# Projection products that read the two token tiles in turn

## The chip, the cores and the metric

The kernel runs on one core of one Trainium2 chip. The time is device microseconds of one execution, given as the median of several runs. Lower is better. A core has TensorE (matrix products, PE in the profile, with its weight loads as PEld), VectorE (DVE), ScalarE (ACT), GpSimd (POOL) and SyncE (SP, which issues most transfers here). Products are written to PSUM, and VectorE and ScalarE read them there.

## The reference

Two decoder layers over 256 tokens of width 1024, and a final RMSNorm. The whole is float32.

```python
h = rms_norm(x, gain)
proj = h @ w_in                       # 1024 x 9808: q, k, v, gate of three mixers, index, merge gates
# three causal mixers, 8 heads of 64 each: a block attention (one block here), an indexer that picks
# the top 64 keys of each query, and forgetting attention; a and b rotate 16 of 64 dims by position
oa, ob, oc = attention_n(q, k, v) * silu(gate)
y = stack([oa, ob, oc]) @ w_branch    # 512 x 1024 each
merged = sum(sigmoid(merge_logit) * y)
x = x + merged @ w_out                # 1024 x 1024
```

## The kernel before

**Numbers in two parts.** Every operand of a product is split into a high part of type fp32r and a rest (`wh`, `wl` for weights; `hTh`, `hTl` for the normalised input; `q`, `bd`, `og` and so on likewise), and a product of two such operands is three products on TensorE: high by high, high by low, low by high. ScalarE makes the high part with a copy, VectorE the rest with a subtraction.

**Two kinds of projection.** For v and the output, `unit_a` has the tokens as the stationary side and 512 weight columns as the moving side. For everything else (q, k, gates, index, merge gates), `unit_b` has 128 weight columns stationary and all 256 tokens moving, so that the result is transposed: features in partitions, tokens in columns. Such a unit is 24 products of 128 x 128 by 256 (8 chunks of the width, three products each) into one PSUM buffer `proj`, of which there are three. `unit_y`, the branch output, is the same with 12 products over `og`. Over both layers there are 130 units of 24 products (two of them with 80 weight columns, `kwf`) and 48 units of 12. All are issued by `mm_ops` (L403); its operands are `hTh[:, k]` or `og[..][:, k]`, 256 consecutive fp32r columns, of which 0 to 127 are the first tile of tokens and 128 to 255 the second.

**Readers of `proj`.** Merge gates: a tanh on ScalarE (L817, L820). Mixer gates: tanh, then a product with `proj` on VectorE (`ev_g`). q and k of mixers a and b and the index: `rope` with two tables from `cst` (`rope_t`), a shuffle and a product on VectorE and two steps on POOL, result in `rr`; then a split, by `split_to` into `q` or by `write_bd` into `bd`, a block-diagonal pair of heads. q and k of mixer c: the split reads PSUM directly. The branch outputs are multiplied with the merge gates into `acc`, which is split into `merged` after the third (`mg`). `kwf` holds the index key and 16 columns that go to `wf`.

**Attention of a pair of heads** (`attend`): the scores `s` (L569 to L571) read `q` by tiles of 128 tokens as stationary side and `bd` as moving side; softmax on VectorE and ScalarE; transposes (L659); products with v into `o` (L674 to L677); then `gated` multiplies `ot` with the gate `g` on POOL or VectorE (L694, L695) and splits into `og`. Scores, masks and transposes are done tile by tile and need tokens in plain order.

**Order.** Nothing is scheduled by the compiler. `Plan.run` replays a list of operations with costs and fixes each engine's order when the program is built; at run time each engine executes its list in that order with semaphores. Weights arrive by DMA into `raw` (three buffers) and are split at L358 (ScalarE) and L362 (VectorE) into rings `wh` and `wl`. At the end stands a block `forms()` whose products go to unused PSUM buffers and reach no output: several ways to read or write a product, after all others on TensorE (L1054 to L1066), beside the final norm's last steps.

The access of the test at L1064, `a` being 128 and `b` two, visits columns 0, 128, 1, 129, ...:

```python
for i in range(4):
    PE.matmul(b2[:, :256].rearrange("p (a b) -> p a b", a=128), w(i), c(i).rearrange("p (b a) -> p a b", a=128), start=True, stop=True)
```

L1054 is the plain read, L1056 a plain read of bf16, L1058 and L1060 read every second column, L1062 every sixteenth, L1066 a plain read from column 8 on.

Of the kernel before, what the change touches and what calls it, by code (L numbers as in the profile page):

```python
# [11 lines left out]
AF = mybir.ActivationFunctionType  # L12
ALU = mybir.AluOpType

L = 2
S = 256
# [3 lines left out]
KC = D // 128  # L20
# [31 lines left out]
def shape_constants():  # L52
    c = np.zeros((128, C_END), np.float32)
    i = np.arange(128)
    c[:, C_ID:C_ID + 128] = np.eye(128)
    c[:, C_UT:C_UT + 128] = i[:, None] <= i[None, :]
    diag = np.where(i[None, :] <= i[:, None], 0.0, MASKED)
    c[:, C_MASK:C_MASK + 128] = diag
    c[:, C_MASK + 256:C_MASK + 384] = diag
    inv = np.power(np.float32(500000.0), -np.arange(0, 16, 2, dtype=np.float32) / np.float32(16))  # L60
    ang = np.arange(S, dtype=np.float32)[None, :] * inv.astype(np.float32)[:, None]
    cos, sin = np.cos(ang).astype(np.float32), np.sin(ang).astype(np.float32)
    ct = np.ones((128, S), np.float32)
    st = np.zeros((128, S), np.float32)
    for b in (0, 64):
        ct[b:b + 8] = cos
        ct[b + 8:b + 16] = cos
        st[b:b + 8] = -sin
        st[b + 8:b + 16] = sin
    c[:, C_ROPE:C_ROPE + 256] = ct  # L70
    c[:, C_ROPE + 256:C_ROPE + 512] = st
    c[:, C_ROPE + 512:C_ROPE + 768] = ct * np.float32(-0.125)
    c[:, C_ROPE + 768:C_ROPE + 1024] = st * np.float32(-0.125)
    return c
# [142 lines left out]
def t_dve(n):  # L217
    return 68.0 + n / 0.96
# [6 lines left out]
def t_pool(n):  # L225
    return 250.0 + 2.2 * n
# [7 lines left out]
def hybrid_trunk(ctx, tc, x, norm_gain, w_in, forget_bias, w_branch, w_out, final_gain, consts, out):  # L234
# [7 lines left out]
    plan = Plan()  # L242
# [7 lines left out]
    def T(b):  # L250
        return b.slot[1]
# [30 lines left out]
    gT = pool.tile([128, L, KC], F32, name="gT")  # L282
    hTh = pool.tile([128, KC, S], F32R, name="hTh")
    hTl = pool.tile([128, KC, S], F32R, name="hTl")
    og = [[pool.tile([128, 4, S], F32R, name=f"og{i}{p}") for p in "hl"] for i in range(2)]
    NBD = 3
    bd = [[pool.tile([128, 2, S], F32R, name=f"bd{i}{p}") for p in "hl"] for i in range(NBD)]
# [127 lines left out]
    def unit_b(name, get, half=0, npart=128):  # L415

        u = unit(name)
        ps = Buf("proj")
        o = lambda: T(ps)[:npart, :S]
        pp = get(u)  # L420
        n = KC // len(pp)
        w = lambda k, i: pp[k // n][i].v[:, k % n, half * 128:half * 128 + npart]
        his = [(lambda k=k: w(k, 0), lambda k=k, h=h: h[:, k], [pp[k // n][0]] + hT_all[i])
               for k in range(KC) for i, h in enumerate((hTh, hTl))]
        los = [(lambda k=k: w(k, 1), lambda k=k: hTh[:, k], [pp[k // n][1]] + hT_all[0]) for k in range(KC)]
        g = his[:8] + los[:4] + his[8:] + los[4:]
        for a, b in ((0, 8), (8, 12), (12, 20), (20, 24)):
            mm_ops(o, g[a:b], t_mm(256), [ps], u, name, a == 0, b == 24, True)
        return u, ps
# [145 lines left out]
    class Pair:  # L575
# [3 lines left out]
        def ev_q(self, ps, key):  # L579
            q = self.q = (Buf("qh"), Buf("ql"))  # L580
            if self.mixer == "c":
                split_to(lambda: T(q[0]), lambda: T(q[1]), lambda: T(ps)[:, :S], S, True, [ps], q[0], q[1], key,
                         -0.125, "q")
            else:
                r = rope(ps, "q", key)
                split_to(lambda: T(q[0]), lambda: T(q[1]), lambda: T(r), S, False, [r], q[0], q[1], key, name="q")

        def ev_k(self, ps, key):
            self.k, self.kt = new_bd()
# [94 lines left out]
        def gated(self):  # L684
            o, g, key = self.o, self.g, self.o_key
            t = Buf("ot")
            kt = [Tok(), Tok()]
            for h in range(2):
                r = slice(64 * h, 64 * h + 64)
                act(lambda r=r, h=h: ACT.activation(T(t)[r], T(o)[64:, h * S:(h + 1) * S], AF.Copy), S, True,  # L690
                    [o], [kt[h]], key, "og", HALF, touch=[t])
                dve(lambda r=r, h=h: DVE.tensor_tensor(T(t)[r], T(o)[:64, h * S:(h + 1) * S], T(t)[r], op=ALU.add),
                    S, [o], [kt[h]], key, "og", t_dve(S) + HALF, touch=[t])
            plan.op([("POOL", t_pool(S), lambda: POOL.tensor_tensor(T(t), T(t), T(g), op=ALU.mult)),  # L694
                     ("DVE", t_dve(S), lambda: DVE.tensor_tensor(T(t), T(t), T(g), op=ALU.mult))],  # L695
                    [g] + kt, [t], key, 0.0, "og").port = True
            gh, gl = og[self.oi]
            split_to(lambda: gh[:, self.p], lambda: gl[:, self.p], lambda: T(t), S, False, [t],
                     k_og[self.oi][0][self.p], k_og[self.oi][1][self.p], key, 0.5, "og")

    def write_bd(src, b, toks, key, ps, shared=False):
        for h in range(2):
            o = slice(64 * h, 64 * h + 64)
            s = (lambda: T(src)[0:64, :S]) if shared else (lambda o=o: T(src)[o, :S])
            hi = lambda o=o, h=h: T(b)[0][o, h]
            lo = lambda o=o, h=h: T(b)[1][o, h]
            act(lambda hi=hi, s=s: ACT.activation(hi(), s(), AF.Copy), S, ps, [src, k_bdz], [toks[h][0]], key, "bd", HALF, touch=[b])
            dve(lambda hi=hi, lo=lo, s=s: DVE.tensor_tensor(lo(), s(), hi().bitcast(F32), op=ALU.subtract), S,
                [src, toks[h][0]], [toks[h][1]], key, "bd", t_dve(S) + HALF, touch=[b], port=not ps)


    def ev_kwf(l, ps, key):
        act(lambda: ACT.activation(wf[64:80], T(ps)[64:80, :S], AF.Copy), S, True, [ps], [k_wf], key, "wf")
        b, toks = new_bd()
        write_bd(rope(ps, "k", key, 64), b, toks, key, False, shared=True)
        return b, toks
# [48 lines left out]
    def index_scores(p, ps, kb, ktoks, key):  # L765
        q = (Buf("qh"), Buf("ql"))
        r = rope(ps, "k", key)
        split_to(lambda: T(q[0]), lambda: T(q[1]), lambda: T(r), S, False, [r], q[0], q[1], key, name="qi")
        s0, s1 = scores(q, kb, ktoks, key + 1)
        base = (p % 2) * 768  # L770
        rel = [tmp6[:, base:base + 256], tmp6[:, base + 256:base + 768]]
# [57 lines left out]
    def unit_y(l, n, j, oi, gates, rank):  # L829
        u = unit(f"y{n}{j}")  # L830
        p = wbr(l, n, j, u)
        ps = Buf("proj")
        gh, gl = og[oi]
        cs = slice((j % 2) * 128, (j % 2) * 128 + 128)
        o = lambda: T(ps)[:, :S]
        g = []
        for k in range(4):
            wh, wl = lambda k=k: p[0].v[:, k, cs], lambda k=k: p[1].v[:, k, cs]
            g += [(wh, lambda k=k: gh[:, k], [p[0], k_og[oi][0][k]]), (wh, lambda k=k: gl[:, k], [p[0], k_og[oi][1][k]]),
                  (wl, lambda k=k: gh[:, k], [p[1], k_og[oi][0][k]])]  # L840
        g = [g[i] for i in (0, 1, 3, 4, 2, 5, 6, 7, 9, 10, 8, 11)]
        for a in (0, 6):
            mm_ops(o, g[a:a + 6], t_mm(256), [ps], u, f"y{n}{j}", a == 0, a == 6, True)
# [11 lines left out]
        if rank == 2:  # L855
            h, lo = merged(j)
            kh, kl = k_mg[j]
            split_to(lambda: h, lambda: lo, lambda: ac, S, False, [k_acc[j]], kh, kl, u, 0.5, "mg")


    DVE.memset(ones, 1.0)
# [181 lines left out]
    def forms():  # L1043

        b = [Buf(t) for t in "sst"]
        f = hTl.rearrange("p k c -> p (k c)")
        fb, gb = f.bitcast(mybir.dt.bfloat16), hTh.rearrange("p k c -> p (k c)").bitcast(mybir.dt.bfloat16)

        def emit():
            b0, b1, b2 = (T(x) for x in b)  # L1050
            w = lambda i: hTh[:, i, :128]
            c = lambda i: f[:, i * 256:i * 256 + 256]
            for i in range(4):
                PE.matmul(b0[:, :256], w(i), c(i), start=True, stop=True)  # L1054
            for i in range(6):
                PE.matmul(b1[:, :256], gb[:, i * 256:i * 256 + 128], fb[:, i * 512:i * 512 + 256], start=True, stop=True)  # L1056
            for i in range(4):
                PE.matmul(b2[:, :256], w(i), f[:, i * 512:(i + 1) * 512].rearrange("p (c t) -> p t c", t=2)[:, 0], start=True, stop=True)  # L1058
            for i in range(4):
                PE.matmul(b0[:, :256].rearrange("p (a b) -> p a b", a=2), w(i), c(i).rearrange("p (b a) -> p a b", a=2), start=True, stop=True)  # L1060
            for i in range(4):
                PE.matmul(b1[:, :256].rearrange("p (a b) -> p a b", a=16), w(i), c(i).rearrange("p (b a) -> p a b", a=16), start=True, stop=True)  # L1062
            for i in range(4):
                PE.matmul(b2[:, :256].rearrange("p (a b) -> p a b", a=128), w(i), c(i).rearrange("p (b a) -> p a b", a=128), start=True, stop=True)  # L1064
            for i in range(4):
                PE.matmul(b0[:, :256], w(i), f[:, i * 256 + 8:i * 256 + 264], start=True, stop=True)  # L1066
        pe(emit, 3400.0, [k_main] + hT_all[0] + hT_all[1], b, 10 ** 6, "forms")
    forms()
    PLAN_T.append(plan)
    PLAN_T[0] = plan.run({"PE": 0.0, "ACT": 0.0, "DVE": 0.0})  # L1070
# [25 lines left out]
```

## Time and profile before

| | |
|---|---|
| median of 3 runs | 636.49 us (635.48 to 637.81) |
| profiled execution | 635.14 us |
| its span | 633.3 us |
| TensorE busy | 624.4 us, 99% |
| VectorE busy | 543.4 us, 86% |
| ScalarE busy | 395.8 us, 62% |
| GpSimd busy | 86.6 us, 14% |
| TensorE's granted clock | full throughout |
| DMA | 105.56 MB, mean 167 GB/s |

A product's row in the profile is its latency, from its first column to its last result; the next product starts long before that, so busy time hides how closely products follow each other. The chain of work that ended last is followed back from the last instruction, at each step to what released it; its pieces have a start, a length and a count. "x<-y" is written and read tile, without buffer numbers. A row of waits names who waited for whom, the sum in us, how often, and the longest.

### The profile page before, as it was taken

The page shows a single profiled execution, that of the slowest core. Times are in us where ns is not written, and L with a number is a line of the kernel's source. Part 1 is how long each engine was busy: PE and PEld are TensorE (multiplying, and loading weights), DVE is VectorE, ACT ScalarE, POOL GpSimd, SP SyncE. Part 2 cuts the span into 40 slices and gives each one's busy share as a digit, 9 for nine tenths or more (in the row PEclk, how much of TensorE's full clock was granted, in tenths as well). Part 3 has the DMA queues.
Part 4 walks back from the last instruction along what each step waited for, and adds up shares of the span by engine and source line. Part 5 has one row for each costly group of instructions (what it writes and reads, how often), then busy time and mean ns, then how long its engine had stood idle before and what let it go on. Part 6 is the DMA issues. An engine that isn't in the chain of part 4 may idle for free.

```text
span 633.3 us, 12633 instructions
## 1 busy us (share of the span) xinstructions
PE 624.4 (99%) x4866; PEld 595.7 (94%) x4866; DVE 543.4 (86%) x1334; ACT 395.8 (62%) x797; POOL 86.6 (14%) x98
## 2 busy tenths in 40 slices
PE   8999989999999999999999999999999999999999
PEld 7999989899998999999889998998999989999988
DVE  8899998976878989899588999979688798989873
ACT  6775476666756667485486656767566574847641
POOL 1332221100000221200004303020000012221001
PEclk9999999999999999999999999999999999999999
DMA  9844637455472562665555544565736454363701
GB/s 300 278 144 148 200 108 258 135 168 172 148 246 68 170 197 67 200 223 177 154 167 166 181 133 154 176 192 166 232 102 201 128 161 148 117 214 102 265 34 67
DMA packets 93853, 105.56 MB, mean 167 GB/s; under 512 B 4320, under 2 KB 82400, under 8 KB 93792
## 3 DMA queue, kind: packets, MB, share of 16 engines
q1 hardware_dynamic: 93504, 104.36, 51.8%
q8 instruction: 38, 0.62, 0.4%
q10 hardware_dynamic: 288, 0.39, 0.2%
q14 instruction: 23, 0.19, 0.1%
HBM read 103.69 MB, written 1.05 MB: 165 GB/s over the span
## 4 chain that ended last, share of the span: by engine, by line
PE 80%; DVE 16%; ACT 2%; DMA 1%; issue 1%; SPq 0%; ACTq 0%; DVEq 0%
PE proj L403 68%; DVE wl L362 6%; PE t L659 2%; DVE isc L804 2%; PE s L569 1%; PE s L571 1%; PE proj L950 1%; PE s L570 1%; DVE t L803 1%; DMA x<-in_x_dram 1%; DVE isc L783 1%; DVE rsh L451 1%; PE o L677 1%; PE o L674 1%; DVE rr L453 1%
## 5 line engine op out<-in xcount | busy, mean ns | idle before, releaser
L362 DVE TENSOR_TENSOR wl<-raw,wh 128x1024 fp32r<-128x1024 f32 (+1 forms) x190 | 235.5, 1251 | 33.0 <-ACT wh L358 31.1
L403 PE MATMUL proj<-hTh,wh 128*128 128x256 f32 (+1 forms) x1040 | 252.1, 278 | 1.1 <-DVE g L598 1.1
L403 PE MATMUL proj<-hTl,wh 128*128 128x256 f32 (+1 forms) x1040 | 250.9, 277 | 0.0
L358 ACT ACTIVATE wh<-raw 128x1024 fp32r<-128x1024 f32 (+1 forms) x190 | 197.9, 1054 | 79.4 <-PE proj L403 58.5
L403 PEld LDWEIGHTS proj<-hTh,wh 128*128 128x128 f32 (+1 forms) x1040 | 194.7, 187 | 2.5 <-DVE g L598 1.6
L403 PEld LDWEIGHTS proj<-hTl,wh 128*128 128x128 f32 (+1 forms) x1040 | 194.6, 187 | 0.8
L403 PE MATMUL proj<-hTh,wl 128*128 128x256 f32 (+1 forms) x1040 | 163.1, 279 | 0.0
L403 PEld LDWEIGHTS proj<-hTh,wl 128*128 128x128 f32 (+1 forms) x1040 | 139.4, 187 | 1.4
L452 POOL TENSOR_TENSOR rsh<-rsh,cst 128x256 f32<-128x256 f32 (+1 forms) x42 | 35.8, 852 | 385.4 <-DVE rsh L451 385.4
L636 ACT ACTIVATE e<-e,st 128x128 f32<-128x128 f32 x96 | 42.6, 445 | 16.8 <-DVE st L632 16.3
L454 POOL TENSOR_TENSOR rr<-rr,rsh 128x256 f32<-128x256 f32 (+1 forms) x42 | 44.0, 1048 | 14.4 <-DVE rr L453 11.6
L403 PE MATMUL proj<-wh,v 128*128 128x512 f32 (+1 forms) x144 | 35.6, 368 | 0.0
L403 PE MATMUL proj<-og0l,wh 128*128 128x256 f32 x128 | 32.7, 279 | 0.0
L403 PE MATMUL proj<-wh,hTh 128*128 128x512 f32 x80 | 32.3, 404 | 0.0
L403 PE MATMUL proj<-og0h,wh 128*128 128x256 f32 x128 | 32.3, 277 | 0.0
L403 PE MATMUL proj<-wh,hTl 128*128 128x512 f32 x80 | 31.5, 393 | 0.0
L690 ACT ACTIVATE ot<-o 64x256 f32<-64x256 f32 x48 | 18.3, 380 | 20.9 <-PE o L677 20.3
L403 PEld LDWEIGHTS proj<-wh,v 128*128 128x128 f32 x144 | 25.2, 188 | 4.7
L664 DVE TENSOR_TENSOR ptl<-t,pth 128x384 fp32r<-128x384 f32 x48 | 25.3, 551 | 0.5
L403 PE MATMUL proj<-og0h,wl 128*128 128x256 f32 x128 | 25.0, 277 | 0.0
L403 PE MATMUL proj<-wl,hTh 128*128 128x512 f32 x80 | 24.9, 392 | 0.0
L647 DVE TENSOR_SCALAR e<-e,st 128x256 f32<-128x256 f32 (+1 forms) x73 | 23.6, 334 | 1.1
(205 smaller groups left out, 1019.1 us busy)
## 6 DMA issues: line engine op xcount, KB each, us to landing
raw<-in_w_in_dram SPq DMA_DIRECT2D x74, 1024.0 KB, 5.2
raw<-in_w_branch_dram SPq DMA_DIRECT2D x24, 512.0 KB, 5.1
raw<-in_w_out_dram SPq DMA_DIRECT2D x8, 1024.0 KB, 5.8
raw<-in_w_in_dram SPq DMA_DIRECT2D x3, 512.0 KB, 7.1
x<-in_x_dram SPq DMA_DIRECT2D x4, 256.0 KB, 4.6
raw<-in_w_in_dram SPq DMA_DIRECT2D x2, 320.0 KB, 5.9
out_dram<-tmp SPq DMA_DIRECT2D x2, 320.0 KB, 2.4
raw<-in_w_in_dram SPq DMA_DIRECT2D x2, 256.0 KB, 3.7
```

The lines of the kernel that those rows point to most:

```text
L358: ACT.activation(p[0].v, sel(c.v), AF.Copy)
L362: DVE.tensor_tensor(p[1].v, sel(c.v), p[0].v.bitcast(F32), op=ALU.subtract)
L403: PE.matmul(o(), a(), b(), start=first and i == 0, stop=last and i == n - 1)
L451: dve(lambda: DVE.stream_shuffle(T(sh)[:np_], a(), SWAP), S, [ps], [sh], key, "rope")
L452: gps(lambda: POOL.tensor_tensor(T(sh)[:np_], T(sh)[:np_], s[:np_], op=ALU.mult), S, [k_rope], [sh], key, "rope")
L454: gps(lambda: POOL.tensor_tensor(T(r)[:np_], T(r)[:np_], T(sh)[:np_], op=ALU.add), S, [sh], [r], key, "rope")
L636: act(lambda t=t, a=a, n=n, e=e, st=st: ACT.activation(T(e)[:, a:a + n], T(e)[:, a:a + n], AF.Exp, bias=T(st)[:, t:t + 1], scale=-1.0, acc ...
L647: DVE.tensor_scalar(T(e)[:, a:a + n], T(e)[:, a:a + n], T(st)[:, 4 + t:5 + t], None, op0=ALU.mult)
L659: PE.transpose(T(ps)[:, i * 128:(i + 1) * 128], T(es[h])[:, i * 128:(i + 1) * 128], ident)
L664: dve(lambda h=h, src=src: DVE.tensor_tensor(T(pl)[:, h], src(), T(ph)[:, h].bitcast(F32), op=ALU.subtract), 384, [ps, kp[h][0]], [kp[h][1 ...
L690: act(lambda r=r, h=h: ACT.activation(T(t)[r], T(o)[64:, h * S:(h + 1) * S], AF.Copy), S, True, [o], [kt[h]], key, "og", HALF, touch=[t])
L804: dve(lambda o=o, t8=t8: DVE.match_replace(o, T(t8), o, TAKEN), n, [t8], [k_isc[i]], key + r * step, "top8")
```

## The change

The 256-token products take the columns of their moving operand in another sequence: column 0 of the first tile, column 0 of the second (128), column 1 of both, and so on (`turns`). The output is written straight ahead, so `proj` holds the tokens in alternating order. What stays elementwise keeps that order (merge gates, `acc`, mixer gates, `rope`, whose tables are permuted when the constants are made). Where tokens have to stand in plain order, the reader takes every second fp32 column, first the even ones, then the odd ones (`tiles`), and writes plainly (`plain`). This goes for the splits into `q`, `bd` and `merged`, for `wf`, and for the gate in the product of `gated`. `unit_a` and attention are as they were. The block at the end has other test products: in `go(m, w, view, k)`, k products with m output columns each read a view of w columns of `hTl`.

Of the diff, `ev_q` shows mixers a and b; mixer c (from PSUM) and `index_scores` are changed alike, and so is the VectorE variant in `gated` and the third operand in `unit_y`.

```diff
+    ct, st = (m.reshape(128, 2, 128).transpose(0, 2, 1).reshape(128, S) for m in (ct, st))
...
+    turns = lambda v: v.rearrange("p (a b) -> p b a", a=2)
+    tiles = lambda v: v.rearrange("p (b a) -> p a b", a=2)
+    plain = lambda v: v.rearrange("p (a b) -> p a b", a=2)
...
     def unit_b(name, get, half=0, npart=128):
...
-        o = lambda: T(ps)[:npart, :S]
+        o = lambda: T(ps)[:npart, :S].rearrange("p (b a) -> p b a", a=2)
...
-        his = [(lambda k=k: w(k, 0), lambda k=k, h=h: h[:, k], [pp[k // n][0]] + hT_all[i])
+        his = [(lambda k=k: w(k, 0), lambda k=k, h=h: turns(h[:, k]), [pp[k // n][0]] + hT_all[i])
...
-        los = [(lambda k=k: w(k, 1), lambda k=k: hTh[:, k], [pp[k // n][1]] + hT_all[0]) for k in range(KC)]
+        los = [(lambda k=k: w(k, 1), lambda k=k: turns(hTh[:, k]), [pp[k // n][1]] + hT_all[0]) for k in range(KC)]
...
         def ev_q(self, ps, key):
...
-                split_to(lambda: T(q[0]), lambda: T(q[1]), lambda: T(r), S, False, [r], q[0], q[1], key, name="q")
+                split_to(lambda: plain(T(q[0])), lambda: plain(T(q[1])), lambda: tiles(T(r)), S, False, [r], q[0], q[1], key, name="q")
...
         def gated(self):
...
-            plan.op([("POOL", t_pool(S), lambda: POOL.tensor_tensor(T(t), T(t), T(g), op=ALU.mult)),
+            plan.op([("POOL", t_pool(S), lambda: POOL.tensor_tensor(plain(T(t)), plain(T(t)), tiles(T(g)), op=ALU.mult)),
...
     def write_bd(src, b, toks, key, ps, shared=False):
...
-            s = (lambda: T(src)[0:64, :S]) if shared else (lambda o=o: T(src)[o, :S])
-            hi = lambda o=o, h=h: T(b)[0][o, h]
-            lo = lambda o=o, h=h: T(b)[1][o, h]
+            s = (lambda: tiles(T(src)[0:64, :S])) if shared else (lambda o=o: tiles(T(src)[o, :S]))
+            hi = lambda o=o, h=h: plain(T(b)[0][o, h])
+            lo = lambda o=o, h=h: plain(T(b)[1][o, h])
...
     def ev_kwf(l, ps, key):
-        act(lambda: ACT.activation(wf[64:80], T(ps)[64:80, :S], AF.Copy), S, True, [ps], [k_wf], key, "wf")
+        act(lambda: ACT.activation(plain(wf[64:80]), tiles(T(ps)[64:80, :S]), AF.Copy), S, True, [ps], [k_wf], key, "wf")
...
     def unit_y(l, n, j, oi, gates, rank):
...
-            g += [(wh, lambda k=k: gh[:, k], [p[0], k_og[oi][0][k]]), (wh, lambda k=k: gl[:, k], [p[0], k_og[oi][1][k]]),
+            g += [(wh, lambda k=k: turns(gh[:, k]), [p[0], k_og[oi][0][k]]), (wh, lambda k=k: turns(gl[:, k]), [p[0], k_og[oi][1][k]]),
...
-            split_to(lambda: h, lambda: lo, lambda: ac, S, False, [k_acc[j]], kh, kl, u, 0.5, "mg")
+            split_to(lambda: plain(h), lambda: plain(lo), lambda: tiles(ac), S, False, [k_acc[j]], kh, kl, u, 0.5, "mg")
...
     def forms():
...
+            go(256, 256, lambda x: x.rearrange("p (a b) -> p b a", a=4), 4)
+            go(256, 256, lambda x: x.rearrange("p (a b) -> p b a", a=8), 4)
+            go(256, 512, lambda x: x.rearrange("p (a b) -> p b a", a=2)[:, :128], 4)
+            go(512, 512, lambda x: x.rearrange("p (a b) -> p b a", a=2), 4)
+            go(512, 512, lambda x: x.rearrange("p (a b) -> p b a", a=4), 4)
+            go(512, 512, lambda x: x.rearrange("p (c a b) -> p c b a", c=2, a=2), 4)
```

The sequence of instructions is the same on every engine up to the block at the end; only access patterns differ. In that block, TensorE's rows are now others. Here are its last rows before (`s`, `t` are PSUM buffers of attention that are free by then):

```order
L403 MATMUL proj_156<-wh_64,v_79 128x256 x4
L403 MATMUL proj_156<-wl_71,v_79 128x256 x2
L1054 MATMUL s_159<-hTl,hTh 128x256 x4
L1056 LDWEIGHTS hTh
L1056 MATMUL s_160<-hTl,hTh 128x256
...
L1058 MATMUL t_161<-hTl,hTh 128x256 x4
L1060 MATMUL s_159<-hTl,hTh 128x256 x4
L1062 MATMUL s_160<-hTl,hTh 128x256 x4
L1064 MATMUL t_161<-hTl,hTh 128x256 x4
L1066 MATMUL s_159<-hTl,hTh 128x256 x4
```

And here are TensorE's last rows now:

```order
L407 MATMUL proj_156<-wh_64,v_79 128x256 x4
L407 MATMUL proj_156<-wl_71,v_79 128x256 x2
L1063 MATMUL s_159<-hTl,hTh 128x256 x4
L1063 MATMUL s_160<-hTl,hTh 128x256 x4
L1063 MATMUL t_161<-hTl,hTh 128x256 x4
L1063 MATMUL s_159<-hTl,hTh 128x512 x4
L1063 MATMUL s_160<-hTl,hTh 128x512 x4
L1063 MATMUL t_161<-hTl,hTh 128x512 x4
```

Thirty products of 256 columns have become twelve of 256 and twelve of 512; they still stand behind all work that the output needs.

More of the change, by code (lines that the diff above doesn't have):

```diff
@@ L581, in ev_q @@
             if self.mixer == "c":
-                split_to(lambda: T(q[0]), lambda: T(q[1]), lambda: T(ps)[:, :S], S, True, [ps], q[0], q[1], key,
-                         -0.125, "q")
+                split_to(lambda: plain(T(q[0])), lambda: plain(T(q[1])), lambda: tiles(T(ps)[:, :S]), S, True, [ps], q[0], q[1],
+                         key, -0.125, "q")
             else:
                 r = rope(ps, "q", key)
-                split_to(lambda: T(q[0]), lambda: T(q[1]), lambda: T(r), S, False, [r], q[0], q[1], key, name="q")
+                split_to(lambda: plain(T(q[0])), lambda: plain(T(q[1])), lambda: tiles(T(r)), S, False, [r], q[0], q[1], key, name="q")
         def ev_k(self, ps, key):
@@ L693, in gated @@
                     S, [o], [kt[h]], key, "og", t_dve(S) + HALF, touch=[t])
-            plan.op([("POOL", t_pool(S), lambda: POOL.tensor_tensor(T(t), T(t), T(g), op=ALU.mult)),
-                     ("DVE", t_dve(S), lambda: DVE.tensor_tensor(T(t), T(t), T(g), op=ALU.mult))],
+            plan.op([("POOL", t_pool(S), lambda: POOL.tensor_tensor(plain(T(t)), plain(T(t)), tiles(T(g)), op=ALU.mult)),
+                     ("DVE", t_dve(S), lambda: DVE.tensor_tensor(plain(T(t)), plain(T(t)), tiles(T(g)), op=ALU.mult))],
                     [g] + kt, [t], key, 0.0, "og").port = True
@@ L767, in index_scores @@
         r = rope(ps, "k", key)
-        split_to(lambda: T(q[0]), lambda: T(q[1]), lambda: T(r), S, False, [r], q[0], q[1], key, name="qi")
+        split_to(lambda: plain(T(q[0])), lambda: plain(T(q[1])), lambda: tiles(T(r)), S, False, [r], q[0], q[1], key, name="qi")
         s0, s1 = scores(q, kb, ktoks, key + 1)
@@ L834, in unit_y @@
         cs = slice((j % 2) * 128, (j % 2) * 128 + 128)
-        o = lambda: T(ps)[:, :S]
+        o = lambda: T(ps)[:, :S].rearrange("p (b a) -> p b a", a=2)
         g = []
@@ L838, in unit_y @@
             wh, wl = lambda k=k: p[0].v[:, k, cs], lambda k=k: p[1].v[:, k, cs]
-            g += [(wh, lambda k=k: gh[:, k], [p[0], k_og[oi][0][k]]), (wh, lambda k=k: gl[:, k], [p[0], k_og[oi][1][k]]),
-                  (wl, lambda k=k: gh[:, k], [p[1], k_og[oi][0][k]])]
+            g += [(wh, lambda k=k: turns(gh[:, k]), [p[0], k_og[oi][0][k]]), (wh, lambda k=k: turns(gl[:, k]), [p[0], k_og[oi][1][k]]),
+                  (wl, lambda k=k: turns(gh[:, k]), [p[1], k_og[oi][0][k]])]
         g = [g[i] for i in (0, 1, 3, 4, 2, 5, 6, 7, 9, 10, 8, 11)]
@@ L1046, in forms @@
         f = hTl.rearrange("p k c -> p (k c)")
-        fb, gb = f.bitcast(mybir.dt.bfloat16), hTh.rearrange("p k c -> p (k c)").bitcast(mybir.dt.bfloat16)
         def emit():
[L1050 to L1066, printed above, removed]
@@ L1067, in forms, with go @@
-        pe(emit, 3400.0, [k_main] + hT_all[0] + hT_all[1], b, 10 ** 6, "forms")
+            bs = [T(x) for x in b]
+            n = 0
+            def go(m, w, v, k):
+                nonlocal n
+                for i in range(k):
+                    x = v(f[:, i * w:(i + 1) * w])
+                    y = x.shape
+                    o = bs[n % 3][:, :m]
+                    o = o.rearrange("p (b a) -> p b a", a=y[2]) if len(y) == 3 else o.rearrange("p (c b a) -> p c b a", b=y[2], a=y[3])
+                    PE.matmul(o, hTh[:, i, :128], x, start=True, stop=True)
+                n += 1
@@ new lines, in emit @@
+            go(256, 256, lambda x: x.rearrange("p (a b) -> p b a", a=4), 4)
[4 more added lines that the diff above has]
+            go(512, 512, lambda x: x.rearrange("p (c a b) -> p c b a", c=2, a=2), 4)
+        pe(emit, 5000.0, [k_main] + hT_all[0] + hT_all[1], b, 10 ** 6, "forms")
```

## The prediction

> **What bounds the kernel now.** I read the page's busy shares first, then the chain of work that ended last.
>
> ```profile
> span 633.3 us, 12633 instructions
> PE 624.4 (99%) x4866; PEld 595.7 (94%) x4866; DVE 543.4 (86%) x1334; ACT 395.8 (62%) x797; POOL 86.6 (14%) x98
> PE 80%; DVE 16%; ACT 2%; DMA 1%; issue 1%; SPq 0%; ACTq 0%; DVEq 0%
> PE proj L403 68%; DVE wl L362 6%; PE t L659 2%; DVE isc L804 2%; PE s L569 1%; PE s L571 1%; PE proj L950 1%; PE s L570 1%; DVE t L803 1%; DMA x<-in_x_dram 1%; DVE isc L783 1%; DVE rsh L451 1%; PE o L677 1%; PE o L674 1%; DVE rr L453 1%
> L403 PE MATMUL proj<-hTh,wh 128*128 128x256 f32 (+1 forms) x1040 | 252.1, 278 | 1.1 <-DVE g L598 1.1
> L403 PE MATMUL proj<-hTl,wh 128*128 128x256 f32 (+1 forms) x1040 | 250.9, 277 | 0.0
> L403 PE MATMUL proj<-hTh,wl 128*128 128x256 f32 (+1 forms) x1040 | 163.1, 279 | 0.0
> L403 PE MATMUL proj<-og0l,wh 128*128 128x256 f32 x128 | 32.7, 279 | 0.0
> ```
>
> TensorE is never idle and L403 alone is 68% of the chain. The means of 277 to 279 ns are latencies of overlapping products. What counts is the distance from one start to the next. The chain's pieces give it: length divided by count.
>
> ```profile
> 98.14 14.07 PE proj L403 x124
> ...
> 318.25 5.55 PE proj L403 x24
> ...
> 336.93 8.41 PE proj L403 x72
> ...
> 394.38 2.83 PE proj L403 x24
> ...
> 404.83 15.43 PE proj L403 x136
> ```
>
> The piece at 318.25 holds 512-column products: 5.55/24 = 231 ns each. The four others are 256-column products: 113.5, 116.8, 117.9 and 113.5 ns, together 40.74/356 = 114.4 ns. There are two paces, about 113.5 and 117.9, the first the commoner. I found no row that says what sets the pace.
>
> The changed products are the three hT groups, 3 x 1040, and those of the branch outputs: 48 units of 12, which are three groups of 128 (og0, one row above) and three of 64 (og1). That is 3120 + 576 = 3696 products, or 3696 x 114.4 = 423 us.
>
> **What the trace shows of the new read.** The block of test products at the end of this very kernel holds the form that the change introduces. L1064 reads columns 0, 128, 1, 129, ... of an fp32r tile and writes straight on, as the new `turns` does. Here are the pieces of the timeline, each cut so that the first product of its group is left out:
>
> ```profile
> 627.10 0.52 PE L1054 MATMUL s<-hTl,hTh 128*128 128x256 f32 x3
> 627.58 0.71 PE L1056 MATMUL s<-hTl,hTh 128*128 128x256 bf16 x5
> 629.24 0.87 PE L1060 MATMUL s<-hTl,hTh 128*128 128x256 f32 x3
> 630.14 0.85 PE L1062 MATMUL s<-hTl,hTh 128*128 128x256 f32 x3
> 630.94 0.50 PE L1064 MATMUL t<-hTl,hTh 128*128 128x256 f32 x3
> ```
>
> A row's length less the last product's own duration, over one less than the count, is the distance. The durations come from the lines' own lists and groups:
>
> ```profile
> L1054 PE MATMUL s<-hTl,hTh x4: 277/282/284, 627.0 to 627.3; 128*128 128x256 f32 x4
> L1056 PE MATMUL s<-hTl,hTh x6: 272/272/283, 627.5 to 628.0; 128*128 128x256 bf16 x6
> L1060 PE MATMUL s<-hTl,hTh x4: 412/412/414, 629.0 to 629.7; 128*128 128x256 f32 x4
> L1062 PE MATMUL s<-hTl,hTh x4: 403/407/408, 629.9 to 630.6; 128*128 128x256 f32 x4
> L1064 PE MATMUL t<-hTl,hTh x4: 275/275/301, 630.8 to 631.2; 128*128 128x256 f32 x4
> ```
>
> Plain read, L1054: (520-277)/2 = 121. bf16, L1056: (710-272)/4 = 109. Steps of 2, L1060: (870-412)/2 = 229. Steps of 16, L1062: (850-407)/2 = 221. The alternating form, L1064: (500-275)/2 = 112; and from its second start (630.94) to the first start of the next group, L1066 (631.27 in the last fence below), there are three distances in 0.33 us, which is 110 to 113. So in one place the alternating read goes at about 112 where the plain read takes 121. I take 111.7.
>
> The Trainium skill, "SBUF — State Buffer", section on the DMA port swizzle, says the contrary: accesses keep full rate only with two hits in a 16-byte line, so alternating columns should be slow and steps of 2 free. The trace has it the other way at both points (112 and 229 ns).
>
> **The sum.** Term 1, the products: 114.4 - 111.7 = 2.7 ns on each of 3696, 10.0 us of TensorE time. Ends: the bf16 distance of 109 (5.4 ns, 20 us) and the slow plain pace of 117.9 (-3.5 ns, -13 us). I take 2.7 because L1064 is the same form, type and size.
>
> Term 2, where TensorE is not the end. In these stretches the chain runs mainly over VectorE:
>
> ```profile
> 48.00:83.00 35.00, 33.37 (x285) 32.80 (x284) 34.86 (x99) 17.43 (x27) 9.45 (x10) 1.00 0.58 179
> 361.00:390.00 29.00, 28.14 (x244) 27.77 (x244) 28.22 (x89) 13.66 (x23) 5.76 (x9) 1.00 0.59 184
> 534.00:563.00 29.00, 29.00 (x250) 28.63 (x248) 26.45 (x71) 20.58 (x46) 6.67 (x8) 1.00 0.33 99
> ```
>
> The columns are length, then busy time and count of PE, PEld, DVE, ACT and POOL. In the first two, VectorE is busy 34.86 of 35.00 and 28.22 of 29.00 us with the index selection; a faster TensorE only waits longer at their end, where it already waits for `bd1l` and `bd2l`:
>
> ```profile
> PE s L571 <- DVE bd1l L708: 1.6, 1, 1.6
> PE proj L403 <- DVE g L598: 1.1, 2, 0.7
> PE s L571 <- DVE bd2l L708: 0.9, 1, 0.9
> ```
>
> These stretches hold 779 products; a fourth like the third, at 240 to 255, adds an estimated 125 by its length. Some 150 of the 904 are attention products and transposes, so about 750 of the changed ones gain nothing. Left: (3696 - 750) x 2.7 = 8.0 us.
>
> Term 3, new waits elsewhere. A unit of 24 products shortens by 62 ns; work timed to finish beneath it loses that cover. The list above shows how few places are tight: the longest wait for `g`, the cover of a gate unit, is 0.7 us. I charge eight more places with one unit's 62 ns: 0.5 us. Ends: 0 and 2.
>
> Term 4, the readers. Now `tiles(...)` takes every second fp32 from PSUM or SBUF: 102 ScalarE copies (q 32, merge 16, split K 52, `wf` 2), 100 VectorE subtractions, and 24 gate products, most of them on VectorE. No row of before shows such a read on these engines. Their rates come from two sizes each:
>
> ```profile
> L664 DVE TENSOR_TENSOR ptl<-t,pth 128x384 fp32r<-128x384 f32 x48 | 25.3, 551 | 0.5
> L662 ACT ACTIVATE pth<-t 128x384 fp32r<-128x384 f32 x48 | 21.8, 481 | 2.9 <-PE t L659 2.8
> L453 DVE TENSOR_TENSOR rr<-proj,cst 128x256 f32<-128x256 f32 x40 | 16.5, 412 | 0.3
> L820 ACT ACTIVATE mth<-proj 128x256 f32<-128x256 f32 x32 | 12.1, 378 | 11.1 <-PE proj L403 10.9
> ```
>
> VectorE takes 128 more columns in 139 ns (0.92 a ns), ScalarE in 103 ns (1.24 a ns). The nearest strided row is L1060: even TensorE's halved rate is 256/229 = 1.12 a ns. VectorE needs less, and ScalarE would lose about 22 ns a copy, 2.2 us on an engine that is busy 62%. I take 0 on the path. Ends: 0, and twice the time per element (rival B). The cosine and sine tables are permuted on the host and cost nothing. No gain is possible from a reader, since none gets shorter.
>
> Term 5, the tail. The final norm's output and the test block end side by side:
>
> ```profile
> 629.62 0.34 SPq L557 DMA_DIRECT2D out_dram<-tmp  x1
> ...
> 631.27 0.64 PE L1066 MATMUL s<-hTl,hTh 128*128 128x256 f32 x4
> ```
>
> The old block starts at 627.0 (L1054 above) and ends at 631.91. The new one has 12 products of 256 and 12 of 512 columns: 12 x 0.112 + 12 x 0.231 = 4.1 us, less than the old 4.9, if all alternating forms are fast. If all go at the step-2 rate, 12 x 0.229 + 12 x 0.46 = 8.3 us, 3.4 later than the old end; perhaps 3 of that would show after the output's landing. The new steps of 64, 32 and 256 columns have no row. I take 0, with 0 to 3 as ends: not below 0, since the output ends last then.
>
> Sum: -8.0 + 0.5 = -7.5 us. The profiled execution took 635.14 us, 1.35 below the median of 636.49; its own time becomes 627.6, the median 629.0. I give 629.0. 0.3%, 1.9 us, is about what a measurement of this kernel can tell from no change.
>
> **Rivals.** A: in the long stream the alternating read has no better pace than plain reads. For it: only three distances of L1064 exist, all behind slow forms, and 112 is barely under the common 113.5. At 113.5 the gain is 2946 x 0.9 = 2.7 us, 634; at 114.4 nothing, 636.5.
>
> B, slower: the readers. If a step-2 read takes VectorE double time (0.27 us for 256 columns) and ScalarE too (0.21), the some 122 changed VectorE instructions add 33 us to 543. In the four stretches of term 2, 108 us where VectorE sets the pace, lies an even share of 108/633, or 5.6 us. In each of the 24 pairs the split of K ahead of the scores grows by 0.21 + 2 x 0.27 = 0.75 us, of which I let 0.4 show: 9.6. Together +15, less 7.5: 644. It decides from about half that penalty. Against it stands the rate argument of term 4.
>
> C: the alternating read reaches the bf16 distance of 109, because what holds plain fp32r back is gone: 2946 x 5.4 = 15.9, less more waits (2 us), gives 622.5. L1064's 112 speaks against it, though it lies between. The Trainium skill, "TensorE: Matmul & The Clock Gate", section "Back-to-back issue gap", gives 262 cycles for 256 columns, an estimated 109.2 ns, which agrees with L1056's 109 and not with either fp32r form.
>
> D, slower: alternating reads fall into the 117.9 pace or worse in the stream. At 117.9: 2946 x 3.5 = +10.3, 647. If each single column out of its neighbours costs what it costs in L1062, 221 ns, it is 3696 x 107 = +395 us, 1032. L1064 contradicts both; the second has 1 in 100. The line rule of the Trainium skill's "SBUF — State Buffer", told above, would have it so.
>
> **Chances.** Forecast 0.50, A 0.20, B 0.09, C 0.12, D 0.09. Faster by over 0.3%: 0.50 + 0.12 + half of A = 0.72. Within 0.3%: the other half of A, 0.10. Slower: B and D, 0.18. The range takes in C and A and ends in front of B's centre: 621.5 to 638.5; the forecast's own is 626 to 632.
>
> **What will show it.** The chain's L403 pieces should come to about 112 a product instead of 113.5 to 117.9, without two paces; `bd`, `qh`, `ql`, `og` and `v` copies should keep their means (L390 and L708 above all); the wait for `bd1l` should grow by up to 0.7 us; the test block should end before the output's landing. The prediction is wrong if the distance stays at 113 or above, or if the `tiles` readers lengthen by more than some 50 ns.

## The result, and the profile after

The changed kernel takes 630.39 us (median of 5 runs, 630.05 to 631.11) against 635.48 us before (5 runs, 634.87 to 637.81): a ratio of 0.9913 with a 95% interval of 0.9893 to 0.9933 (the two medians alone give 0.9920). By the medians that is 5.1 us less, by the ratio 5.5; 7.5 were forecast. Its profiled execution took 630.21 us.

Busy shares and the chain that ended last, from the changed kernel's page (`mm_ops` is now L407, the weights' split L362 and L366):

```profile
span 628.4 us, 12640 instructions
PE 615.5 (98%) x4860; PEld 584.3 (93%) x4860; DVE 543.7 (87%) x1334; ACT 400.0 (64%) x797; POOL 85.4 (14%) x98
PE 71%; DVE 21%; ACT 4%; DMA 2%; issue 1%; SPq 0%; ACTq 0%; DVEq 0%
PE proj L407 61%; DVE wl L366 8%; PE t L663 2%; ACT e L640 2%; DVE isc L808 2%; PE proj L954 2%; DVE t L807 1%; DMA raw<-in_w_out_dram 1%; PE s L573 1%; PE s L575 1%; PE s L574 1%; DVE rsh L455 1%; DVE rr L457 1%; DVE isc L787 1%; DVE e L636 1%
```

TensorE's part of the chain fell from 80% to 71%, VectorE's rose from 16% to 21%. ScalarE is busy 4.2 us more. The pieces of the chain that answer to those shown of before:

```profile
97.79 13.85 PE proj L407 x124
...
316.44 5.55 PE proj L407 x24
...
334.86 8.23 PE proj L407 x72
...
391.85 2.68 PE proj L407 x24
...
401.97 15.18 PE proj L407 x136
```

The products of 512 columns (second row) are where they were, 231 ns. Those of 256 are at 111.7, 111.7 and 111.6 ns in the first, fourth and fifth row; before, the fourth was at 117.9. The third, 114.3 against 116.8, also holds the whole length of its last product, 0.28 us, and is no pace: without it the two are 112.0 and 114.5. The second pace is gone but for some 40 products. Over the distances between the starts of all such products in the two traces, those under 130 ns have a mean of 111.7 ns, against 114.6 before; what is 130 ns and above, the waits, adds up to 12.8 us against 9.9. The list of waits shows some of these:

```profile
PE s L575 <- DVE bd1l L712: 2.0, 1, 2.0
PE proj L407 <- DVE g L602: 1.7, 2, 0.9
PE proj L954 <- DVE small L478: 1.6, 1, 1.6
PE s L575 <- DVE bd2l L712: 1.3, 1, 1.3
PE t L663 <- DVE e L651: 1.2, 5, 0.3
...
PE proj L407 <- DVE rr L457: 0.4, 2, 0.2
```

The two ends of the index selection grew by 0.4 us each (`bd1l`, 1.6 before; `bd2l`, 0.9), the wait for `g` by 0.6. Before, the transposes waited once for `e`, the numbers of the softmax, and nothing in the list waited for `rr`:

```profile
PE t L659 <- DVE e L647: 0.3, 1, 0.3
```

The readers: ScalarE's copies in the kernel before, then in the changed one (mean ns behind the comma):

```profile
L389 ACT ACTIVATE qh<-rr 128x256 fp32r<-128x256 f32 x24 | 9.7, 410 | 1.4 <-POOL rr L454 1.3
L393 ACT ACTIVATE v<-acc 128x256 fp32r<-128x256 f32 x16 | 6.3, 416 | 8.6 <-DVE acc L853 8.6
L393 ACT ACTIVATE qh<-proj 128x256 fp32r<-128x256 f32 x8 | 3.0, 374 | 2.5 <-PE proj L403 2.4
```

```profile
L393 ACT ACTIVATE qh<-rr 128x256 fp32r<-128x256 f32 x24 | 11.4, 479 | 2.0 <-POOL rr L458 1.7
L397 ACT ACTIVATE v<-acc 128x256 fp32r<-128x256 f32 x16 | 7.2, 474 | 10.1 <-DVE acc L857 10.1
L397 ACT ACTIVATE qh<-proj 128x256 fp32r<-128x256 f32 x8 | 3.0, 374 | 2.0 <-PE proj L407 1.9
L699 DVE TENSOR_TENSOR ot<-ot,g 128x256 f32<-128x256 f32 x22 | 9.9, 450 | 0.2
```

From PSUM a step of 2 costs nothing (374 and 374). From SBUF it costs ScalarE 58 to 69 ns, and VectorE's gate product 30 (420 before). VectorE's subtraction from `rr` (`ql`) went from 455 to 468 ns.

### The profile page after: what moved, and what is told of

It reads as the page before. It is cut to its first block, busy times and chain, and to the rows that moved or that the text cites. A ratio compares the mean times of both kernels' runs of the same rounds, so it can differ in the third digit from the quotient of the medians.

```text
span 628.4 us, 12640 instructions
## 1 busy us (share of the span) xinstructions
PE 615.5 (98%) x4860; PEld 584.3 (93%) x4860; DVE 543.7 (87%) x1334; ACT 400.0 (64%) x797; POOL 85.4 (14%) x98
## 4 chain that ended last, share of the span: by engine, by line
PE 71%; DVE 21%; ACT 4%; DMA 2%; issue 1%; SPq 0%; ACTq 0%; DVEq 0%
PE proj L407 61%; DVE wl L366 8%; PE t L663 2%; ACT e L640 2%; DVE isc L808 2%; PE proj L954 2%; DVE t L807 1%; DMA raw<-in_w_out_dram 1%; PE s L573 1%; PE s L575 1%; PE s L574 1%; DVE rsh L455 1%; DVE rr L457 1%; DVE isc L787 1%; DVE e L636 1%
## 5 line engine op out<-in xcount | busy, mean ns | idle before, releaser
L366 DVE TENSOR_TENSOR wl<-raw,wh 128x1024 fp32r<-128x1024 f32 (+1 forms) x190 | 234.7, 1247 | 30.9 <-ACT wh L362 29.7
L407 PE MATMUL proj<-hTh,wh 128*128 128x256 f32 (+1 forms) x1040 | 247.0, 277 | 2.1 <-DVE g L602 1.7
L407 PE MATMUL proj<-hTl,wh 128*128 128x256 f32 (+1 forms) x1040 | 245.7, 275 | 0.0
L362 ACT ACTIVATE wh<-raw 128x1024 fp32r<-128x1024 f32 (+1 forms) x190 | 197.8, 1055 | 71.2 <-PE proj L407 49.1
L407 PEld LDWEIGHTS proj<-hTh,wh 128*128 128x128 f32 (+1 forms) x1040 | 199.0, 191 | 3.9 <-DVE g L602 2.5
L407 PEld LDWEIGHTS proj<-hTl,wh 128*128 128x128 f32 (+1 forms) x1040 | 199.2, 192 | 0.7
L407 PE MATMUL proj<-hTh,wl 128*128 128x256 f32 (+1 forms) x1040 | 160.1, 277 | 0.0
L407 PEld LDWEIGHTS proj<-hTh,wl 128*128 128x128 f32 (+1 forms) x1040 | 137.9, 191 | 1.3
L407 PE MATMUL proj<-wh,v 128*128 128x512 f32 (+1 forms) x144 | 35.6, 368 | 0.0
L407 PE MATMUL proj<-og0l,wh 128*128 128x256 f32 x128 | 32.2, 277 | 0.3 <-DVE og0l L398 0.3
L407 PE MATMUL proj<-wh,hTh 128*128 128x512 f32 x80 | 32.3, 404 | 0.0
L407 PE MATMUL proj<-og0h,wh 128*128 128x256 f32 x128 | 32.1, 277 | 0.0
L407 PE MATMUL proj<-wh,hTl 128*128 128x512 f32 x80 | 31.5, 394 | 0.0
L407 PEld LDWEIGHTS proj<-wh,v 128*128 128x128 f32 x144 | 25.2, 188 | 4.7
L663 PE MATMUL t<-cst,e 128*128 128x128 f32 x144 | 24.5, 279 | 1.8 <-DVE e L651 1.2
L407 PEld LDWEIGHTS proj<-og0l,wh 128*128 128x128 f32 x128 | 24.6, 192 | 0.7 <-DVE og0l L398 0.5
L407 PE MATMUL proj<-wl,hTh 128*128 128x512 f32 x80 | 24.9, 392 | 0.0
```

Source lines behind the costliest of these rows:

```text
L362: ACT.activation(p[0].v, sel(c.v), AF.Copy)
L366: DVE.tensor_tensor(p[1].v, sel(c.v), p[0].v.bitcast(F32), op=ALU.subtract)
L407: PE.matmul(o(), a(), b(), start=first and i == 0, stop=last and i == n - 1)
L663: PE.transpose(T(ps)[:, i * 128:(i + 1) * 128], T(es[h])[:, i * 128:(i + 1) * 128], ident)
```

## The experiments

All times are medians. Kernels that ran together share their runs of the kernel before, 635.5 to 635.7 us.

**The products alone.** In the changed kernel, `tiles` becomes a straight read:

```diff
-    tiles = lambda v: v.rearrange("p (b a) -> p a b", a=2)
+    tiles = lambda v: v.rearrange("p (a b) -> p a b", a=2)
```

> The products alternate as in the changed kernel, but every reader takes its columns straight on, so tokens stand in the wrong order from there on (the time of every other step stays). Theory T (the change gains 8.4 us in the distances between product starts, and gives part back because ScalarE's 76 copies that read every second fp32 column of SBUF take 55 to 69 ns longer, ahead of the scores): without those readers 628 to 629.3 us, 1 to 2.4 less than the changed kernel's 630.4. Rival R (the readers cost nothing on the path; what is missing is lost where VectorE sets the pace): 630 to 630.8, as the changed kernel. Products at 111.6 ns in both.

Measured: 629.23 us (628.02 to 630.19), 0.9889 [0.9869, 0.9910] of before. Its median lies in T's span, but the interval reaches that of the changed kernel. Two of its executions and four of the changed kernel's (with those of the repeat below) had the full clock throughout: 628.02 and 628.05 us against 629.70 to 630.21, which speaks for T.

**The readers alone.**

```diff
-    turns = lambda v: v.rearrange("p (a b) -> p b a", a=2)
+    turns = lambda v: v.rearrange("p (b a) -> p b a", a=2)
```

> The products read straight on as before, but the readers take every second column as in the changed kernel (tokens in the wrong order). T: 636.5 to 638, 1 to 2.4 above the kernel before (635.5), with the ScalarE copies from SBUF at 466 to 480 ns. R: 635 to 636. Products at two paces, 113.3 and about 118 ns, in both.

Measured: 635.52 us (635.09 to 638.22), 0.9998 [0.9986, 1.0010]. R's number, and T's was missed. But the copies, too, came out otherwise than T said. Their row here:

```profile
L393 ACT ACTIVATE qh<-rr 128x256 fp32r<-128x256 f32 x24 | 10.2, 431 | 1.6 <-POOL rr L458 1.5
```

They took 431 ns, 21 more than before and not 69. The same reads are dearer while TensorE's reads alternate (479).

**The order restored at PSUM.** The tables stay unpermuted, and the first reader of each `proj` takes the tokens in order; nothing reads SBUF with a step of 2:

```diff
-        a = lambda: T(ps)[:np_, :S]
-        dve(lambda: DVE.stream_shuffle(T(sh)[:np_], a(), SWAP), S, [ps], [sh], key, "rope")
+        a = lambda: tiles(T(ps)[:np_, :S])
+        dve(lambda: DVE.stream_shuffle(plain(T(sh)[:np_]), a(), SWAP), S, [ps], [sh], key, "rope")
...
-            act(lambda: ACT.activation(acc[:, j], T(ps)[:, :S], AF.Tanh, scale=0.5), S, True, [ps], [k_acc[j]], u, "mth")
+            act(lambda: ACT.activation(plain(acc[:, j]), tiles(T(ps)[:, :S]), AF.Tanh, scale=0.5), S, True, [ps], [k_acc[j]], u, "mth")
```

> The products alternate; the order of tokens is restored by whoever reads PSUM (shuffle, rope product, tanh, the gate products), so nothing reads SBUF with a step of 2. T, with the changed kernel's trace, where step-2 reads of PSUM took ScalarE 374 and 378 ns and VectorE 418 to 421 ns as before: 628 to 629.3, the same as with the products alone. R: 630 to 630.8. A third outcome: the shuffle or the rope product of VectorE slows with a step-2 read of PSUM, by over 50 ns each, and the time is above 630.4.

Measured: 628.23 us (627.78 to 628.78), 0.9880 [0.9862, 0.9897], as T expected. Its copies from `rr`, shuffles and gate products:

```profile
L392 ACT ACTIVATE qh<-rr 128x256 fp32r<-128x256 f32 x24 | 9.8, 411 | 2.0 <-POOL rr L457 1.7
L454 DVE STREAM_SHUFFLE rsh<-proj 128x256 f32<-128x256 f32 x40 | 18.0, 449 | 0.2
L698 DVE TENSOR_TENSOR ot<-ot,g 128x256 f32<-128x256 f32 x22 | 9.2, 420 | 0.2
```

Plain copies from SBUF are at 411 ns beside alternating products, so most of the cost, 48 of 69 ns, needs the two together; a shuffle that reads PSUM with a step of 2 is at 449 (448 before).

**The changed kernel again**, unedited.

> The changed kernel once more, beside the others of this call. T (its ScalarE copies from SBUF cost 1 to 2 us of the path, though they cost the kernel before nothing): 630 to 631, ratio 0.990 to 0.993, above the 628.2 of the version that restores the order at PSUM. R (no cost): 628 to 629.5, ratio 0.988 to 0.990.

Measured: 630.11 us (629.70 to 631.96), 0.9916 [0.9902, 0.9929]. Its interval lies wholly above that of the version that restores the order at PSUM (0.9862 to 0.9897): reading SBUF with a step of 2 costs the changed kernel some 1.9 us, though it costs the kernel before nothing that could be measured.

**The rope path alone restored at PSUM.** The edit of `rope` from above in the changed kernel, with the splits behind it reading straight on; mixer gates and the merge stay as changed.

> The changed kernel, but the shuffle and the rope product restore the order as they read PSUM, so the splits of q and K ahead of the scores read SBUF straight on again. Merge and mixer gates stay in alternating order: 16 ScalarE copies, 16 VectorE subtractions and 24 gate products still read SBUF with a step of 2. If the price is paid ahead of the scores (T): 628 to 629, as with everything restored at PSUM (628.2). If it is paid by the gates and the merge: 629.5 to 630.5, as the changed kernel (630.1).

Measured: 628.64 us (628.32 to 630.77), 0.9895 [0.9877, 0.9912]. By the medians 1.5 of the 1.9 us are back, as T expected; the interval reaches that of the changed kernel, so the times alone don't settle it. The waits do. One for `e` is left, and none for `rr`, as before and as with everything restored at PSUM:

```profile
PE t L662 <- DVE e L650: 0.3, 1, 0.3
```

That is 1.3 us of waits less than in the changed kernel. Four copies from `rr` into `bd` stand on the changed kernel's chain (the first at 226.07 us, 0.45 us long), and none on this one's. So the price is paid mainly on the way from `rr` to the scores and their softmax.

**The index selection cut short.** In the kernel before and in the version that restores at PSUM, one round of the search instead of eight (the selected keys are others):

```diff
-        for r in range(8):
+        for r in range(1):
```

> The kernel before with one of the eight rounds of the index selection's search for the largest scores on VectorE (14 rounds of two tiles less over both layers). Theory S (in the selection's stretches at 48 to 83 and 361 to 390 us VectorE sets the pace, and TensorE waits 2.5 us at their ends): 631 to 634, since TensorE is nearly continuous anyway; it is here as the base of the next.

> The version that restores the order at PSUM, with one of the eight rounds. S: without the selection's load the alternating products gain in these stretches too, so its distance to the kernel before with one round is 8.5 to 10 us instead of the 7.4 with eight. Rival: the selection isn't what holds it; the distance stays 7 to 8 us.

Measured: 632.0 us (631.34 to 633.53) and 623.09 us (622.59 to 624.77); 0.9942 [0.9929, 0.9955] and 0.9804 [0.9789, 0.9819] of the kernel before. The distance is 8.9 us where it was 7.4 with eight rounds, as S said, though the intervals of the two distances overlap. The traces decide it: no wait for `bd1l` or `bd2l` is left in either list, and from the first to the last product of the two selection stretches the alternating version gains 1.9 us on the plain one, where the changed kernel gained 0.1 on the kernel before. (With one round, some products stand in another order than with eight, the same in both versions.) The chains by engine, of the first and of the second:

```profile
PE 89%; DVE 7%; DMA 2%; ACT 1%; issue 1%; POOL 0%; DVEq 0%; ACTq 0%
```

```profile
PE 82%; DVE 10%; ACT 4%; DMA 1%; issue 1%; POOL 1%; SPq 0%; ACTq 0%
```

With VectorE relieved, the chain is mostly TensorE's again, and more of the shorter distance arrives.

**The products of 512 columns as well.** In `unit_a` and `first_v` the moving weights alternate between their halves, and the readers of PSUM restore:

```diff
-                wh = lambda p=p, k=k: p[0].v[:, k % 2, c:c + n]
+                wh = lambda p=p, k=k: turns(p[0].v[:, k % 2, c:c + n])
...
-                    dve(lambda o=o, ps=ps, n=n: DVE.tensor_tensor(o, o, T(ps)[:, :n], op=ALU.add), n, [ps], [k_x[t][hh]],
+                    dve(lambda o=o, ps=ps, n=n: DVE.tensor_tensor(plain(o), plain(o), tiles(T(ps)[:, :n]), op=ALU.add), n, [ps], [k_x[t][hh]],
```

> As the one before, and the products of 512 columns (v and output projections) alternate between the halves of their weight columns too, restored by the readers of PSUM. In the changed kernel's test block this form had 215 to 217 ns against 231 plain: 456 x 15 = 6.8 us of TensorE time. If most of it lies on the path (T4): 622 to 625. If these units wait for weights or splits anyway (R4): within 1.5 us of the one before.

Measured: 623.20 us (622.63 to 625.21), 0.9806 [0.9784, 0.9828]: 5.0 us of the 6.8 arrive, as T4 has it. The timeline has six products from the start of the first row to that of the third:

```profile
309.82 1.03 PE L406 MATMUL proj<-wh,v 128*128 128x512 f32 x4
310.68 0.59 PE L406 MATMUL proj<-wl,v 128*128 128x512 f32 x2
311.11 1.03 PE L406 MATMUL proj<-wh,v 128*128 128x512 f32 x4
```

That is 1.29/6 = 215 ns instead of 231.

**Low parts of K last in the scores**, on top of that:

```diff
                 PE.matmul(o, ql[:, sl], kh[:, :, :n], start=False, stop=False)
+            for o, sl, n in parts:
                 PE.matmul(o, qh[:, sl], kl[:, :, :n], start=False, stop=True)
```

> The version with 512-column products alternating too (623.2 us), and in the scores the products with the low part of K come after all others of both tiles, which gives VectorE's split of K two products of 512 columns (0.46 us) more before TensorE waits for it. If those waits hold the path (1.8 and 1.2 us at the ends of the selection, and small ones): 621.5 to 622.7. Rival: VectorE is the end there and TensorE's later wait changes nothing: 622.8 to 623.6.

Measured: 623.23 us (622.28 to 624.91), the rival's number: no change.

**The scores alternate too**, with the order of the products as in the last one:

```diff
-            parts = [(o.rearrange("p (h c) -> p h c", h=2), sl, n) for o, sl, n in
+            parts = [(o.rearrange("p (c h) -> p c h", h=2), sl, [v[:, :, :n].rearrange("p h c -> p c h") for v in (kh, kl)])
```

> As the one before, and the products of the scores alternate between the two heads' columns of K, with softmax and index reading PSUM with a step of 2: 96 x (231 - 216) + 96 x (118 - 112) = 2.0 us of TensorE time. If the path has them: 1 to 2 us under the one before. If VectorE's maximum slows with a step of 2, or the scores lie where VectorE sets the pace: within 0.8 us of it.

Measured: 621.56 us (621.54 to 621.64), 0.9779 [0.9764, 0.9793]. By the medians it is 1.7 us under the version with the low parts last, whose interval (0.9789 to 0.9826) just meets its own, and the fastest of all: 13.9 us under the kernel that the study began with.

**What the new read needs: the distance of the pairs.** One execution, with products like this in the block at the end, d being 2, 4, 8, 16, 32 and 64:

```diff
+                go(lambda x: x.rearrange("p (g a b) -> p g b a", a=2, b=d), 8)
```

> The version that restores the order at PSUM, with another block at the end: eight products of 256 columns each, first plain, then alternating in pairs 2, 4, 8, 16, 32 and 64 columns apart, then plain again. Theory L (a read is slow where a 16-byte line gives fewer than two columns before the next line is needed, unless two lines are held open): pairs 2 apart go at 112 or below, and all others at 112 too. Theory B (what matters is that consecutive columns come from different banks, some power of two apart): slow, 220 ns and more, up to some distance, and 112 from there. Plain products 113 to 121 in both.

The timeline has pairs 2, 4 and 64 apart, and the second plain group (the first row lacks its group's first product):

```profile
621.53 1.00 PE L1063 MATMUL s<-hTl,hTh 128*128 128x256 f32 x7
...
622.37 1.06 PE L1063 MATMUL t<-hTl,hTh 128*128 128x256 f32 x8
...
625.95 1.06 PE L1063 MATMUL s<-hTl,hTh 128*128 128x256 f32 x8
626.84 1.12 PE L1063 MATMUL s<-hTl,hTh 128*128 128x256 f32 x8
```

With 275 to 283 ns for the last product: 120 ns for pairs 2 apart, 112 for 4 and 64 (8, 16 and 32 were the same), 120 for plain. Neither theory holds. L missed the pair of 2, B the slow range. Pairs 2 apart stay within four neighbouring columns; pairs 4 apart alternate between two such groups. So 4 apart is enough for the 112, and 2 is not; that the groups are the reason is a guess that no run tested.

**What the weights have to do with it.** One execution, with every second weight column loaded in some groups (`first` reads the weights straight on, `even` every second column; `same` reads the moving columns straight on):

```diff
+            go(first, same, 8)
+            go(even, same, 8)
+            go(even, turns, 8)
+            go(first, turns, 8)
```

> The version that restores the order at PSUM, with another block at the end: eight products of 256 columns each, with weights read straight on or every second column, and moving columns straight on or alternating. Theory W (plain products are held at 113 to 121 ns because the weight read beside them disturbs the moving read, which alternating columns escape): weights with a step of 2 take twice the reads, so plain moving columns go to 125 ns or more beside them and alternating ones stay near 112. Rival M (the pace is a matter of the moving read alone): the step of the weights changes neither, 117 to 121 and 112.

Here are the second, third and fourth group, each without its first product:

```profile
620.78 1.00 PE L1063 MATMUL s<-hTl,hTh 128*128 128x256 f32 x7
...
621.74 1.00 PE L1063 MATMUL t<-hTl,hTh 128*128 128x256 f32 x7
...
622.68 0.94 PE L1063 MATMUL s<-hTl,hTh 128*128 128x256 f32 x7
```

(1.00 - 0.28)/6 = 120 ns for plain moving columns beside stepped weights, the same as beside plain ones; 120 for alternating columns beside stepped weights; and 111 beside plain weights. Again neither: stepped weights don't slow plain products, but they take the whole advantage from alternating ones. So the pace belongs to both reads together, and why is left open.

## Why the prediction was right, point by point

The time lies in the range and the step that carries the gain, the shorter distance, is there. But 630.39 looks nearer to the forecast 629.0 than it is: the forecast started from 636.49, and the kernel before came out at 635.48 over five executions. Against the forecast of 7.5 us less, a quarter to a third is missing, and one sign of being wrong that the prediction named did appear (term 4).

**Term 1, the products: 10.0 us forecast.** Right, and a little small: 114.6 - 111.7 = 2.9 ns on 3696 products, 10.7 us. Three distances in a test block, taken behind slow forms, stood for all 3696. On the other side the 114.4 was partly luck: the 116.8 among its four pieces holds a last product's whole length and is no pace. Rivals A, C and D are out: the pace of plain reads, the 109 of bf16 and the 117.9 were not met.

**Term 2, VectorE's stretches: 2.0 us of it lost.** Right. In the kernel before and in the version with the rope path restored, both profiled at full clock, the four stretches hold the same 822 changed products, where 750 were estimated. At 2.9 ns each they should gain 2.4 us; by the starts of the same products they gain nothing. The shortened selection shows the cause in two of the stretches, and by the medians gives 1.5 us back. In the version without reads of SBUF by steps, all losses come to 10.7 - 7.4 = 3.3 us, where terms 2 and 3 had 2.5. The wait for `bd1l` grew by 0.4 us, where up to 0.7 was announced. That nothing is gained when TensorE needs the split of K later (low parts last) fits.

**Term 3, new waits: 0.5 us.** Too small: of the 3.3 us, 0.9 are left for it. The wait for `g` alone grew by 0.6 us. (The growth at `e`, from 0.3 to 1.2 us, belongs to term 4, since it goes with the rope path's reads.) The chain's move to VectorE, 16% to 21%, fits. The working has a slip, 24 x 2.7 being 65 ns and not 62; the 0.5 stands.

**Term 4, the readers: 0 us.** This is the step that failed, by 1.9 us (630.11 against 628.23), and the prediction's own sign of it is met: the copies from SBUF lengthened by more than 50 ns, and `ql` and `bd` copies did not keep their means. The bound of 22 ns a copy was taken from the rate of TensorE's own strided read. PSUM and SBUF were put together in it: a step of 2 is free from PSUM on both engines, and dear from SBUF on ScalarE, 58 to 69 ns. And the full price is paid only beside alternating products (21 ns beside plain ones), which no row of before could show. Rival B had the right place, the copies ahead of the scores, at a third of its price: 69 ns where it took 0.21 us. The double time on VectorE, most of its sum, was not met: 13 ns on `ql`, 30 on the gate product.

**Term 5, the tail: 0.** Right. In the changed kernel the last products of the block start at 626.6 us, with the span's end at 628.4; two columns 256 apart, 512 in all, go at 215 to 217 ns, and more than two in turn are slow (four at 138 to 144, eight at 222).

So from 7.5: the products gave 0.7 more, terms 2 and 3 took 0.8 more, the readers 1.9. That comes to 5.5, between the 5.1 first measured and the 5.6 of the repeat.

## What to carry to other kernels

Where fp32r products follow each other on TensorE without a pause, read the moving columns from two places in turn, at least four columns apart, with the weights read straight on, and let whoever reads PSUM restore the order; there it is free, and in SBUF it is not. Price a changed access pattern beside the load that the change itself creates, not in the kernel as it was. And count a faster bound engine only where it is the end of the chain: here 7.4 of 10.7 us arrived, and 8.9 with VectorE relieved.

## What the runs showed of the hardware that was not expected

- **TensorE's alternating reads slow ScalarE's copies from SBUF only when these read with a step:** a copy of 256 columns took 410 ns (plain, plain products), 431 (step of 2, plain products), 411 (plain, alternating products), 479 (both). TensorE's distances were 111.7 ns beside either kind of copy. Why is open.
- **TensorE's clock was halved after waits of under 2 us.** The changed kernel's two profiled executions differ in the stretch that follows the wait for `bd1l` (2.0 and 1.9 us). First the one of the result, then the one of the repeat; the column behind POOL is the granted clock:

```profile
80.00:85.00 5.00, 4.77 (x37) 4.46 (x37) 4.87 (x22) 2.00 (x9) 1.49 (x2) 1.00 0.68 213
```

```profile
80.00:85.00 5.00, 4.02 (x18) 3.73 (x19) 4.87 (x20) 1.97 (x7) 2.12 (x3) 0.66 0.68 213
```

In the repeat the clock was at half for 3.4 us there, and once more at 13 to 16 us; products of 256 columns stood 213 ns apart, and the span was 630.1 us instead of 628.4. Four of the other timed versions showed one or two such windows in their profile, the kernel before none. But of the kernel before, too, nine of 35 executions among the experiments had a mean granted clock of 0.997, against six of ten of the changed kernel at 0.995 or 0.997. Such windows are in the times of both; that longer waits make them likelier isn't shown, and which waits bring them about wasn't tried.
